# One transformer block in fp32: 256-token halves for the first weight tiles, earlier places for the scans' first chunk, and other PSUM banks in the output projections

## The chip, the core and the metric

The kernel runs on one core of a Trainium2 chip. Times are microseconds of the device for one execution. The five engines of the core are TensorE (PE, matmuls and transposes), VectorE (DVE), ScalarE (ACT), GpSimd (POOL) and SyncE (SP, which issues the transfers). Lower is better; what counts is the median of several runs.

## What is computed

The reference is one layer on 1024 tokens of width 1024, batch 1, all in float32. Each of its three sub-layers is wrapped in two RMS norms, and its result is added to the residual stream:

```
h = rms_norm(x, g_mix_pre);  proj = h @ w_in          # q, k, v of both mixers, gates, decays
attn_o = window_attention(rope(aq), rope(ak), av)     # 8 heads of 64, 2 kv heads, +-128 tokens
dn_o   = gated_deltanet(conv(dqkv), dgate, ...)       # 4 heads of 128, forward and backward scan
x = x + rms_norm(concat(attn_o, dn_o) @ w_out, g_mix_post)
c = cross_attention(rms_norm(x), rms_norm(mem), w_cq, w_ckv) @ w_co   # 4 heads of 256, 256 memory tokens
x = x + rms_norm(c, g_cross_post)
x = x + rms_norm((silu(gate) * up) @ w_down, g_ffn_post)              # gate, up = rms_norm(x) @ w_gate_up
```

## The kernel before

Float32 products are made of three matmuls of a rounded format (fp32r): every operand is split into `hi` (a cast, on ACT) and `lo` (source minus `hi`, on DVE or GpSimd), and hi\*hi, hi\*lo and lo\*hi are summed in PSUM. `split` (lines 100 to 107) makes the two halves; L103 and L104 of the profile are its cast and its subtraction, whoever calls it. `load_w` (line 119) loads one weight tile (`wraw`, 512 KB) and splits it to `whi`, `wlo`; its pool has two buffers of each. Tokens are worked on in two halves of 512 (`HALF`), each of four tiles of 128.

The order in which the engines' instructions stand is set by a scheduler from the program's order, its dependencies and its buffers. It may put matmuls of a later part between those of an earlier part, as far as their PSUM banks and weight buffers are free in program order. Each engine then works off its own list in order.

**Phase 1**, from 0 to about 368 us. Eight tiles of x are loaded (six buffers `xt`, L205; the last two when a buffer is free, L217), squared on ACT (L220), scaled on DVE (L223), transposed on PE (L228) and split to `hT`, per half `hhi` and `hlo`. `gemm_b` (L260) then multiplies weight tiles of `w_in` with `hT`, 512 tokens per matmul: 8 k-tiles of 3 matmuls for each weight tile and half. The first two weight tiles (`ws`, `pps`) are those of the DeltaNet's k. The convolution, the rotary embedding, the DeltaNet's solves (L602 to L625) and, between them, the window attention (scores `psw` L653, exponentials `sc` L662, transposes `ptw` L679, casts `ph` and differences `pl`, products `pow` L684) follow. The rotary tables `sinT` and `cosT` live in a pool of their own (`rt`); `sn` and `rot` of the rotary products in `trp`. What the scans need is written to DRAM (`d_kv`, `d_pz`, `d_gate`).

**The scans**, from about 369 to 520 us. `scan(g)` for two pairs of heads goes through eight chunks, forward and backward in the same step. Each step loads `kv` (L813, 512 KB each) and `pz` (L814, 256 KB each), two buffers of each in a pool `t3` that comes into being when phase 1 is over, and at its end `gate` (L872). Its matmuls are `psc` (L805). The rest of the window attention, the memory's norm (`mt`, squared at L911 and scaled at L914, transposed at L921, split to `mT`) and the product of `w_ckv` with it (`pck` L936, `pcv` L952) stand between the steps.

**The output projections.** `mid_gemm` (line 1019) multiplies one half of the tokens with `w_out`, later with `w_co`: twice (`ch`) 512 output columns, four token tiles `t` each with a PSUM bank of its own (`pmg`, L1036), and the weights in four pieces (`kp`). Each bank is emptied by ACT (L1039, sum of squares) and DVE (L1040, times the gain, to `z`). After both column halves every token tile is normed, added to the residual (L1050), squared (L1053) and scaled by its next norm's factor (L1056, ACT). PSUM's eight banks are here four `pg` (pool `pg3`), two `pn` (transposes) and two `px`. The calls in program order are: `w_out` on half 0, `w_out` on half 1, `cross_q` and `cross_attention` on half 0, then on half 1, `w_co` on half 0, `w_co` on half 1, and the feed-forward part (`pA` and others, L1211).

**cross_attention** (line 1105) goes through four heads. The scores of four token tiles (`pcs`, L1117, 24 matmuls of 256 columns) go to two `px` banks; DVE takes the maximum (L1119), ACT the exponentials (L1124), DVE the reciprocal and the product (L1126, L1127). Eight transposes (`pct`, L1133) go to two `pn` banks and are split to `cph`, `cpl`; twelve matmuls (`pco`, L1143) fill two `px` banks, which are split back into the operand. In the attention of half 0 the scheduler has put products of `cross_q` for half 1 (`pcq`) between these steps, in that of half 1 products of `w_co` (`pmg`), for half 0 and, beside the last heads, for half 1 as far as its k-tiles are done.

The banks of mid_gemm are claimed in one line, which is the same for both column halves:

```python
            pp = [pg.tile([P, 512], F32, tag="pg", name="pmg") for _ in range(4)]
```

## Time and profile before

| what | value |
|---|---|
| median of 3 runs | 1551.01 us (1550.01 to 1552.21) |
| the profiled execution | 1550.21 us |
| its span, first to last instruction | 1548.5 us (1.7 us lie around it) |
| mean granted PE clock | 0.991 |
| PE, DVE, ACT, POOL busy | 1491.4, 1057.6, 753.9, 364.7 us |
| moved by the transfers | 242.96 MB, 157 GB/s on average |

A timeline row gives an instruction's start, its length, engine, line, operation, tile written and tiles read, and its shape; in brackets stands how long the engine was idle ahead of it and what it waited for. Lengths of matmuls in a row overlap: a pace is read from start to start. A row of a stretch gives each engine's busy time in it, the clock that PE was granted (1.00 is full, 0.50 half), the share of time that the transfer engines were busy, and GB/s. At the start of the trace the clock column does not tell the state, the matmuls' lengths do.

### The profile page before, as it was taken

Reading aid. Unit: us, or ns where it says so; the run is one execution under the profiler, and the core shown is the slowest. Engines: PE = TensorE matmul, PEld = TensorE weight load, DVE = VectorE, ACT = ScalarE, POOL = GpSimd, SP = SyncE. Lnnn points to the kernel's source line nnn. Section 1 sums busy time; section 2 is a strip of 40 time slices with the busy share of each in tenths; the row PEclk is TensorE's granted clock in tenths of the full one; section 3 lists DMA queues with packets and bytes.
Section 4 is the critical chain, followed back from the end, with each engine's and each line's share of the span. In section 5 each row is a group of like instructions: output and inputs, shape, how many; then the busy total and the mean of one; then the engine's idle time right before and its main releaser. Section 6 shows DMA issues by size and latency. Waiting matters only on the chain. (4 is left out here: it accounts for less than half of the span.)

```text
span 1548.5 us, 21052 instructions
## 1 busy us (share of the span) xinstructions
PE 1491.4 (96%) x7451; PEld 1251.4 (81%) x7451; DVE 1057.6 (68%) x1712; ACT 753.9 (49%) x1536; POOL 364.7 (24%) x364
## 2 busy tenths in 40 slices
PE   6999999998899999999999999999999999999998
PEld 5888887777899777788888777888888888888786
DVE  6868999686798855444346368786868554696665
ACT  5578733256558865454336575332323332454532
POOL 2020200011237202053102221443533433000021
PEclk9999999999999999999999999999999999999999
DMA  6244575646997764354213254344433334853355
GB/s 205 75 116 138 157 205 136 180 138 178 338 285 250 230 227 162 99 187 144 74 55 123 88 198 143 114 131 129 150 119 120 102 103 146 292 188 102 109 175 165
DMA packets 264710, 242.96 MB, mean 157 GB/s; under 512 B 33800, under 2 KB 203677, under 8 KB 264605
## 3 DMA queue, kind: packets, MB, share of 16 engines
q1 hardware_dynamic: 264605, 241.62, 49.6%
q8 instruction: 59, 0.97, 0.3%
q14 instruction: 46, 0.38, 0.1%
HBM read 172.07 MB, written 66.88 MB: 154 GB/s over the span
## 5 line engine op out<-in xcount | busy, mean ns | idle before, releaser
L103 ACT CAST whi<-wraw 128x1024 fp32r<-128x1024 f32 x108 | 113.2, 1049 | 147.9 <-PE pmg L1036 33.9
L104 DVE TENSOR_TENSOR wlo<-wraw,whi 128x1024 fp32r<-128x1024 f32 x70 | 87.1, 1246 | 86.3 <-ACT whi L103 80.4
L260 PE MATMUL pg<-hhi,whi 128*128 128x512 f32 x352 | 140.3, 399 | 0.0
L260 PE MATMUL pg<-hlo,whi 128*128 128x512 f32 x352 | 139.6, 397 | 0.0
L260 PE MATMUL pg<-hhi,wlo 128*128 128x512 f32 x352 | 138.6, 394 | 0.0
L104 POOL TENSOR_TENSOR wlo<-wraw,whi 128x1024 fp32r<-128x1024 f32 x38 | 92.3, 2430 | 175.3 <-ACT whi L103 175.2
L1036 PE MATMUL pmg<-whi,b 128*128 128x512 f32 x384 | 119.6, 398 | 2.6 <-ACT whi L103 2.2
L1211 PE MATMUL pA<-s,whi 128*128 128x512 f32 x352 | 109.5, 392 | 1.4 <-ACT m L1228 1.4
L1036 PEld LDWEIGHTS pmg<-whi,b 128*128 128x128 f32 x384 | 71.9, 190 | 18.2 <-ACT whi L103 2.7
L1211 PEld LDWEIGHTS pA<-s,whi 128*128 128x128 f32 x352 | 65.3, 188 | 15.1 <-ACT m L1228 2.0
L1401 PE MATMUL pdX<-dhl,whi 128*128 128x512 f32 x264 | 76.1, 390 | 1.5 <-DVE zv L1456 0.8
L260 PEld LDWEIGHTS pg<-hhi,whi 128*128 128x128 f32 x352 | 66.7, 190 | 13.2 <-ACT hhi L103 0.2
L260 PEld LDWEIGHTS pg<-hhi,wlo 128*128 128x128 f32 x352 | 66.6, 189 | 13.3
L260 PEld LDWEIGHTS pg<-hlo,whi 128*128 128x128 f32 x352 | 66.6, 189 | 12.7
L1036 PE MATMUL pmg<-wlo,b 128*128 128x512 f32 x192 | 71.9, 394 | 0.0
L1288 POOL TENSOR_TENSOR act<-act,up 128x512 f32<-128x512 f32 x33 | 50.1, 1519 | 89.8 <-DVE up L1287 53.1
L1211 PE MATMUL pA<-s,wlo 128*128 128x512 f32 x176 | 68.7, 391 | 1.9 <-DVE wlo L104 1.9
L103 ACT CAST whi<-araw 128x1024 fp32r<-128x1024 f32 (+1 forms) x36 | 35.3, 982 | 70.5 <-PE pdX L1401 27.6
L104 DVE TENSOR_TENSOR wlo<-araw,whi 128x1024 fp32r<-128x1024 f32 (+1 forms) x36 | 40.7, 1132 | 38.9 <-ACT whi L103 38.8
L285 DVE SCALAR_TENSOR_TENSOR acc<-cp,cols,acc 128x1024 f32<-128x1024 f32 x48 | 62.0, 1294 | 0.1
L1401 PEld LDWEIGHTS pdX<-dhl,whi 128*128 128x128 f32 x264 | 49.3, 188 | 12.7 <-issue 1.1
L1260 POOL TENSOR_TENSOR sr<-wraw 128x512 f32<-128x512 f32 x22 | 29.4, 1336 | 124.9 <-DMA wraw<-in_w_gate_up_dram 124.2
(413 smaller groups left out, 4067.0 us busy)
## 6 DMA issues: line engine op xcount, KB each, us to landing
wraw<-in_w_gate_up_dram SPq DMA_DIRECT2D x52, 512.0 KB, 3.8
kv<-d_kv SPq DMA_DIRECT2D x32, 512.0 KB, 7.1
wraw<-in_w_in_dram SPq DMA_DIRECT2D x22, 512.0 KB, 5.5
b<-in_w_down_dram SPq DMA_DIRECT2D x20, 512.0 KB, 7.0
araw<-d_as SPq DMA_DIRECT2D x20, 512.0 KB, 3.7
pz<-d_pz SPq DMA_DIRECT2D x32, 256.0 KB, 6.5
wraw<-in_w_ckv_dram SPq DMA_DIRECT2D x16, 512.0 KB, 5.0
wraw<-in_w_out_dram SPq DMA_DIRECT2D x16, 512.0 KB, 3.9
```

What stands on the lines that cost most here:

```text
L103: nc.scalar.copy(hi, src)
L104: (eng or nc.vector).tensor_tensor(lo, src, f32(hi), ALU.subtract)
L260: nc.tensor.matmul(p_, w[:, k, :], ah[a][:, k, :], start=(k == 0 and i == 0), stop=(k == nk - 1 and i == 2))
L285: nc.vector.scalar_tensor_tensor(acc, cp[:, t:t + S], taps[t], acc, ALU.mult, ALU.add)
L1036: nc.tensor.matmul(pp[t], act[a][:, k, tt], w_[:, kk, :], start=(k == 0 and i == 0), stop=(k == KT - 1 and i == 2))
L1211: nc.tensor.matmul(out_, w[a][:, k, :], xx[b_][:, k, :], start=(start and k == 0 and i == 0), stop=(k == HK - 1 and i == 2), skip_group_ch ...
L1260: nc.gpsimd.tensor_tensor(s[0], b_[:, 0:HK], b_[:, HK:], ALU.add)
L1288: nc.gpsimd.tensor_tensor(o_, o_, up, ALU.mult)
L1401: nc.tensor.matmul(banks[t], a[:, k - k0, tt], w, start=(first and k == 0 and i == 0), stop=(k == NB - 1 and i == 2), skip_group_check=not ...
```

## The change

- The tiles `xt` have eight buffers, and all eight loads of x are issued together.
- The first two weight tiles are multiplied with half 0 of the tokens in two passes of 256 tokens, so 96 matmuls of 256 columns stand where 48 of 512 did. Half 1 is done as before.
- The rotary tables become one tile `sct` of a pool `ra` that lives through the scans, and `sn`, `rot` (and `vT`) use a tag `rr` in it. In even steps `pz` takes a place of `rr`, and in even steps of the first pair of heads `kv` takes the place of the tables; in odd steps one buffer each remains in `t3`. For the second pair of heads `kv` stays as it was.
- The loads of `gate` are ordered behind the `kv` load of the step before.
- `mid_gemm` claims its second column half's banks from `px` twice and `pg` twice, for `w_out` on half 0 from `px` twice and `pn` twice.
- L1056 becomes a multiplication on DVE (1075 in the changed file).

```diff
-    xts = [t1.tile([P, D], F32, tag="xt", name="xt", bufs=6) for _ in range(6)]
+    xts = [t1.tile([P, D], F32, tag="xt", name="xt", bufs=8) for _ in range(NT)]
...
-            gemm_b(*ws[i], hT[hf:hf + 1], [pps[i][hf]])
+            if hf:
+                gemm_b(*ws[i], hT[1:2], [pps[i][1]])
+
+        for o in (() if hf else (slice(0, 256), slice(256, 512))):
+            for i in range(2):
+                gemm_b(*ws[i], [[t[:, :, o] for t in hT[0]]], [pps[i][0][:, o]])
...
-    sinT = rt.tile([P, S], F32, name="sinT")
-    cosT = rt.tile([P, S], F32, name="cosT")
+    sct = ra.tile([P, 2, S], F32, tag="sct", name="sct")
+    sinT, cosT = sct[:, 0], sct[:, 1]
...
-            pz, kv = tl("pz", [P, 2, 2, 2, P]), tl("kv", [P, 2, 2, 4, P])
+            near = step % 2 == 0
+            pz = (ra.tile([P, 2, 2, 2, P], F32, tag="rr", name="pz", bufs=2) if near else tl("pz", [P, 2, 2, 2, P], bufs=1))
+            if g == 0:
+                kv = (ra.tile([P, 2, 2, 4, P], F32, tag="sct", name="kv") if near else tl("kv", [P, 2, 2, 4, P], bufs=1))
+            else:
+                kv = tl("kv", [P, 2, 2, 4, P])
+            before = loaded
             for d in range(2):
-                nc.sync.dma_start(kv[:, d], d_kv[g][cs[d]])
+                loaded = nc.sync.dma_start(kv[:, d], d_kv[g][cs[d]])
...
+                with tc.issue_after(before.ins):
+                    nc.sync.dma_start(gt[:, d], d_gate[rows_, cs[d] * P:(cs[d] + 1) * P]
...
+    PG, PN, PX = (pg, "pg"), (pn, "pn"), (px, "px")
+
+    def mid_gemm(tz, act, w, gp, res, dst, hf, between=None, banks=([PG] * 4, [PX] * 2 + [PG] * 2)):
...
-            pp = [pg.tile([P, 512], F32, tag="pg", name="pmg") for _ in range(4)]
+            pp = [q_.tile([P, 512], F32, tag=t_, name="pmg") for q_, t_ in banks[ch]]
...
-            nc.scalar.activation(xr, z, AF.Identity, scale=r2)
+            nc.vector.tensor_scalar(xr, z, r2, None, ALU.mult)
...
-    xn0 = mid_gemm(tz, mxT[0], w_out, gp, x, d_x1, 0)
+    xn0 = mid_gemm(tz, mxT[0], w_out, gp, x, d_x1, 0, banks=([PG] * 4, [PX] * 2 + [PN] * 2))
```

The scheduler's new order at three places. First PE's list at its very start, before: transposes of x (`ps`, L228) and the first products (L260).

```order
L228 MATMUL ps<-ident,xt 128x128 x32
L260 MATMUL pg<-hhi_142,whi 128x512 x2
L228 MATMUL ps<-ident,xt 128x128 x16
L260 MATMUL pg<-hlo_143,whi 128x512
L260 MATMUL pg<-hhi_142,wlo 128x512
L260 MATMUL pg<-hhi_142,whi 128x512
```

The same place in the changed kernel, where the two lines are 227 and 259:

```order
L227 MATMUL ps<-ident,xt 128x128 x16
L259 MATMUL pg<-hhi_146,whi 128x256
L227 MATMUL ps<-ident,xt 128x128 x8
L259 MATMUL pg<-hhi_146,whi 128x256
L259 MATMUL pg<-hlo_147,whi 128x256
L259 MATMUL pg<-hhi_146,wlo 128x256
```

Before, PE transposes four token tiles and then multiplies; now one product stands behind the second tile, and fourteen (the first three are shown) behind the third, with the fourth tile's transposes after them.

Second, ACT's list at the first steps of the scans, before. `whi` is the first weight tile of `w_ckv`, `khi` the cast of the keys' second half, `sc` the exponentials of the window attention, `ph` the cast of transposed probabilities.

```order
L835 COPY vn<-psc 128x512
L644 CAST qs<-qr 128x512
L103 CAST whi<-wraw 128x1024
L103 CAST khi<-kraw 128x1024
L662 ACTIVATE sc,ssum<-sc,nm 128x384 x4
L666 ACTIVATE es<-es 128x4
L103 CAST ph<-ptw 128x512
```

And in the changed kernel, where the lines of `vn`, `sc` and `es` are 849, 666 and 670:

```order
L103 CAST ph<-ptw 128x512
L670 ACTIVATE es<-es 128x4
L849 COPY vn<-psc 128x512
L666 ACTIVATE sc,ssum<-sc,nm 128x384 x4
L103 CAST whi<-wraw 128x1024
L868 COPY of<-psc 128x512
L103 CAST khi<-kraw 128x1024
```

The two casts have moved behind the four exponentials. A little ahead of this place, the two squares of `mt` (L911) have moved as well, from ahead of a table load and four exponentials to a place behind them and behind one more `ph`. In SP's list eight `kv` and eight `pz` loads now precede the first load of `w_ckv`, where four of each did; two of these kv and four of these pz loads stand among the last stores of phase 1.

Third, PE's list in the cross attention of half 1, at the third of its four heads, before: `pct` are the transposes of the probabilities, `pmg` the products of `w_co`.

```order
L1036 MATMUL pmg<-whi,b_6973 128x512
L1036 MATMUL pmg<-whi,b_6974 128x512
L1133 MATMUL pct<-ident,cpr 128x128 x8
L1036 MATMUL pmg<-wlo,b_6973 128x512
L1036 MATMUL pmg<-whi,b_6973 128x512
L1036 MATMUL pmg<-whi,b_6974 128x512
```

And in the changed kernel at its third head, where L1136, L1152 and L1162 are the lines of `pcs`, `pct` and `pco`:

```order
L1136 MATMUL pcs<-kr_6189,b_7589 128x256
L1136 MATMUL pcs<-kr_6190,b_7588 128x256
L1152 MATMUL pct<-ident,cpr 128x128 x8
L1162 MATMUL pco<-cph,vr_6191 128x512 x2
L1162 MATMUL pco<-cpl,vr_6191 128x512
L1162 MATMUL pco<-cph,vr_6192 128x512
```

Before, 30-odd products of `w_co` stand between a head's scores and its transposes, and some twenty between these and its output; now nothing does, for the last three of the four heads. Behind the last head 117 products of `w_co` follow in a row.

More of the change, by code (lines that the diff above doesn't have):

```diff
@@ L144, in tile_hybrid_block @@
     nega = sm.tile([P, 8], F32, name="nega")
+    ra = p12.enter_context(pool("ra", 1, side="right"))
     p1 = ExitStack()
     hx = p1.enter_context(pool("hx", 1, side="right"))
-    rt = p1.enter_context(pool("rt", 1, side="right"))
     trp = p1.enter_context(pool("trp", 2, side="right"))
@@ L198, in small @@
         return ps.tile([P, 512], F32, tag="ps", name="ps")
-    xts = [t1.tile([P, D], F32, tag="xt", name="xt", bufs=6) for _ in range(6)]
+    xts = [t1.tile([P, D], F32, tag="xt", name="xt", bufs=8) for _ in range(NT)]
     gmix = t1.tile([P, D], F32, tag="gmix", name="gmix", bufs=1)
     xload = []
-    for t in range(6):
+    for t in range(NT):
         xload.append(nc.sync.dma_start(xts[t], x[t * P:(t + 1) * P, :]))
@@ L214, in tile_hybrid_block @@
             t = 4 * hf + j
-            xt = xts[t] if t < 6 else t1.tile([P, D], F32, tag="xt", name="xt", bufs=6)
-            if t >= 6:
-                nc.sync.dma_start(xt, x[t * P:(t + 1) * P, :])
+            xt = xts[t]
             junk = t1.tile([P, D], F32, tag="junk", name="junk", bufs=1)
@@ L742, in tile_hybrid_block, with pair @@
     tl_ = p1.enter_context(pool("tl", 2))
+    def pair():
+        t = ra.tile([P, 2, HALF], F32, tag="rr", name="rr", bufs=2)
+        return t[:, 0], t[:, 1]
     def attn_proj(ct):
@@ L749, in attn_proj @@
             rop = trp.tile([P, HALF], F32, tag="rop", name="rop")
-            sn = trp.tile([P, HALF], F32, tag="rot", name="sn")
-            rot = trp.tile([P, HALF], F32, tag="rot2", name="rot2")
+            sn, rot = pair()
             nc.vector.tensor_tensor(sn, pp[hf], sinT[:, sl], ALU.mult)
@@ L764, in value_proj @@
         for hf in range(2):
-            vT = trp.tile([P, HALF], F32, tag="rot", name="vT")
+            vT = pair()[0]
             nc.scalar.copy(vT, pp[hf])
@@ L805, in mm @@
                 nc.tensor.matmul(out[:, d, h, :], lt[:, d, h, :], rt[:, d, h, :], start=True, stop=True)
-        st, first, late = None, [], None
+        st, first, late, loaded = None, [], None, None
         for step in range(NT):
```

3 lines of the change are left out of this document (1 added, 2 removed).

## The prediction

> **What bounds the kernel now.** I read the page, then TensorE's waits, then the timeline around each wait that the change touches. The page's first part:
>
> ```profile
> PE 1491.4 (96%) x7451; PEld 1251.4 (81%) x7451; DVE 1057.6 (68%) x1712; ACT 753.9 (49%) x1536; POOL 364.7 (24%) x364
> ```
>
> TensorE (PE) is busy 96% of the span, so time can come from two things alone: PE's idle time (1548.5 - 1491.4 = 57 us) and the stretches in which it runs at half clock. Which waits make up the idle time is told by PE's waits (us in total, times, longest):
>
> ```profile
> PE ps L228 <- DVE xt L223: 12.7, 4, 8.2
> PE pow L684 <- ACT ph L103: 7.3, 4, 4.0
> PE pmg L1036 <- DVE z L1040: 2.4, 1, 2.4
> PE pmg L1036 <- ACT whi L103: 2.2, 1, 2.2
> PE pA L1211 <- DVE wlo L104: 1.9, 3, 0.8
> PE pA L1211 <- ACT m L1228: 1.4, 2, 0.7
> PE pco L1143 <- ACT cph L103: 1.0, 2, 0.5
> PE pco L1143 <- DVE cpl L104: 0.8, 2, 0.6
> ```
>
> The first row is the start, the second the start of the scans, the third and fourth the output projections, the fifth and sixth the stretch right after them. The last two lie in the cross attention of the second half of the tokens. The change works at every one of these places: at the first four to remove waits, at the last, as its order of instructions shows, to add some.
>
> **The start.** PE's timeline (start, length):
>
> ```profile
> 16.13 4.03 PE L228 MATMUL ps<-ident,xt 128*128 128x128 f32 x16 [2.32 <-DVE xt L223]
> 19.99 1.22 PE L260 MATMUL pg<-hhi,whi 128*128 128x512 f32 x2
> 21.75 3.87 PE L228 MATMUL ps<-ident,xt 128*128 128x128 f32 x16 [0.54 <-DVE xt L223]
> 25.70 0.40 PE L260 MATMUL pg<-hhi,wlo 128*128 128x512 f32 x1
> 25.93 0.40 PE L260 MATMUL pg<-hhi,whi 128*128 128x512 f32 x1
> ```
>
> From 16.13 on, PE waits only 0.54 us. In the changed order one 256-token matmul stands ahead of the third token tile's transposes and fourteen behind them, so the 2.32 us wait takes one matmul (about 0.2 us) and the 0.54 us goes. The 48 matmuls of 0.23 us (25.70 to 25.93) become 96 of 0.12 (24 in 2.9 us, the row at 754.22 below): 11.5 against 11.0, a loss of 0.5. That leaves 0.3 us. At 19.99 two matmuls take 1.22 us, half speed; at 25.70 the clock is up. If PE without the 0.54 us hole gets it up one 3.4 us stretch earlier (the length of such a stretch is that of the half-clock row at 622.70 below), that is worth 1.7 more. I take half of it. The two token loads that go earlier are waited for by no PE row. **Start: 1.2 us gained**; ends -0.5 (extra instructions alone) and 2.0.
>
> **The scans' first chunk.** PE, then ACT, SP's queue, and the stretches (PE busy, PEld, DVE, ACT, POOL, granted clock, DMA share, GB/s):
>
> ```profile
> 371.42 0.49 PE L684 MATMUL pow<-ph,vhl 128*128 128x512 f32 x1 [2.00 <-ACT ph L103]
> 392.36 0.79 PE L684 MATMUL pow<-ph,vhl 128*128 128x512 f32 x1 [4.00 <-ACT ph L103]
> 394.57 0.77 PE L936 MATMUL pck<-mT,whi 128*128 128x256 f32 x2
> ```
>
> ```profile
> 371.39 1.28 ACT L662 ACT_TABLE_LOAD   x1
> 372.68 0.62 ACT L662 ACTIVATE sc<-sc,nm 128x384 f32<-128x384 f32 x1
> 375.19 1.04 ACT L103 CAST ph<-ptw 128x512 fp32r<-128x512 f32 x2
> 376.13 1.56 ACT L106 ACTIVATE mT<-ptm,cols 128x256 fp32r<-128x256 f32 x4
> 387.00 1.04 ACT L103 CAST whi<-wraw 128x1024 fp32r<-128x1024 f32 x1 [4.05 <-DMA wraw<-in_w_ckv_dram]
> ```
>
> ```profile
> 376.79 0.59 SPq L126 DMA_DIRECT2D wraw<-in_w_ckv_dram  x1
> ```
>
> ```profile
> 390.60:397.40 6.80, 5.04 (x22) 4.85 (x23) 2.94 (x8) 3.74 (x10) 0.00 (x0) 0.50 1.06 366
> 400.00:440.00 40.00, 39.02 (x315) 37.31 (x314) 35.56 (x103) 19.25 (x44) 12.44 (x9) 1.00 1.00 326
> ```
>
> The loads' sizes, from the page's DMA issues:
>
> ```profile
> kv<-d_kv SPq DMA_DIRECT2D x32, 512.0 KB, 7.1
> pz<-d_pz SPq DMA_DIRECT2D x32, 256.0 KB, 6.5
> ```
>
> ACT takes its instructions in order. It stands 4.05 us at the cast of `w_ckv`'s first tile, whose load, issued at 376.79, queues behind the scans' loads; the exponentials that PE needs stand behind that cast, so PE idles 4.00 us and then runs 6.8 us at clock 0.50. In the changed order the cast stands behind these exponentials, and the squares of `mem` behind the first ones. How early can the first `w_ckv` matmul (394.57 now) come? Ahead of the table load at 371.39 stand now two squares of 1.05 (the size of the cast at 387.00) and a `ph` of 0.5, so ACT is free for this chain at 368.8. Ahead of the cast and with it now stand a table load 1.28, eight exponentials at 0.6 (4.8), the two squares 2.1, five `ph` at 0.5, eight `mT` at 0.39, four copies of 0.5, and the cast 1.04: 16.9 us, so 385.7 if ACT never waits. I allow 2 us of waits for PE's products, 387.7. But the load comes later too: eight kv and eight pz loads, not four and four, precede it, of which two kv and four pz are issued before the last waits of phase 1. That leaves 4 MB ahead of it instead of 3, and 1 MB at 326 to 366 GB/s is 3 us. If it is issued when it is now it lands between 387 and 390; with the queue the emptier for what went early I take 388, and the matmul comes at about 389: 5.5 us earlier. From 400 on PE is busy 39.02 of 40 us, so the gain is kept. The half clock costs 1.4 us behind 394.57 now; PE's new idle time ahead of 388 puts the clock down there as well, so I count nothing. The rotary products use the new places before the loads fill them, and the load of each gate, moved behind a kv load, is needed only at the end of a step. **Scans: 5.5 us gained**; ends 0 (the loads set the pace) and 9 (5.5, the 2.00 us wait and the half clock).
>
> **The output projections.** Stretches, then ACT and DVE:
>
> ```profile
> 587.00:590.50 3.50, 3.50 (x17) 2.89 (x16) 2.31 (x3) 0.55 (x2) 0.00 (x0) 1.00 0.37 104
> 619.30:622.70 3.40, 1.17 (x6) 0.93 (x6) 1.12 (x1) 3.19 (x4) 0.13 (x1) 1.00 0.00 0
> 622.70:626.10 3.40, 3.40 (x10) 2.63 (x9) 1.24 (x2) 0.00 (x0) 0.00 (x0) 0.50 0.46 161
> ```
>
> ```profile
> 618.43 2.19 ACT L1056 ACTIVATE xr<-z,pr 128x1024 f32<-128x1024 f32 x2
> ```
>
> ```profile
> 371.28 0.75 DVE L914 TENSOR_SCALAR mt<-mt,mrs 128x1024 f32<-128x1024 f32 x1 [2.36 <-POOL mrs L161]
> ```
>
> In `w_out`'s first half the second 512 columns take px and pn, which are free, in place of pg banks that wait for L1040: 2.4 us go, less about 0.4 for a `wlo` that is next late. In its second half PE waits 2.2 us for a `whi` cast that queues behind the L1056 scalings on ACT, and 3.4 us at clock 0.50 follow, which cost 1.7. With L1056 on DVE, which is busy 1.12 of the 3.40 us, all that goes. Sixteen scalings of 0.75 cost DVE 12 us, priced at the like row L914. 2.0 + 2.2 + 1.7 = 5.9; I take **5.5 us gained**; ends 2 and 6.3. The pA waits (3.3 us) come while ACT still holds L1053 and L1056 of `w_co`'s first half; four scalings of 1.1 us leave it. **1.5 us gained**; ends 0 and 3.3.
>
> **What the banks take away.** `w_co` is what PE now does between the steps of the second half's cross attention, nearly all of it for the first half. Its second 512 columns now want px, which cross_attention uses for scores and output and which comes earlier in the program. So they cannot start until the attention is over, and the order shows three heads back to back without one other matmul. What a head takes can be read where filler hides it now:
>
> ```profile
> 754.22 3.04 PE L1117 MATMUL pcs<-kr,b 128*128 128x256 f32 x24
> 757.29 0.69 DVE L1119 TENSOR_REDUCE cmx<-pcs 128x2 f32<-128x512 f32 x1 [0.54 <-PE pcs L1117]
> 758.75 0.47 ACT L1124 ACTIVATE cpr<-pcs,cmx 128x256 f32<-128x256 f32 x1
> 759.54 0.69 DVE L1127 TENSOR_TENSOR cpr<-cpr,csum 128x512 f32<-128x512 f32 x1
> 763.24 0.60 PE L1133 MATMUL pct<-ident,cpr 128*128 128x128 f32 x4
> 764.57 1.08 ACT L103 CAST cph<-pct 128x512 fp32r<-128x512 f32 x2 [1.82 <-PE pct L1133]
> 765.18 1.29 DVE L104 TENSOR_TENSOR cpl<-pct,cph 128x512 fp32r<-128x512 f32 x2 [1.06 <-ACT cph L103]
> 772.84 0.59 ACT L103 CAST b<-pco 128x512 fp32r<-128x512 f32 x1 [0.58 <-PE pco L1143]
> ```
>
> Scores end at 757.26; maximum, exponentials and division end at 759.54 + 0.69 = 760.23: PE idles 3.0 us. Then come eight transposes, and the first `cpl` ends 0.61 + 0.69 = 1.3 us after the first `cph` starts; one matmul of 0.2 fits in: 1.1 idle. The next head's scores need the bank of the first output, split in 0.59 and about 0.7 (as for a `cpl`), 1.3 us, while the second output's six matmuls run 1.4: 0.1. That is 4.2 us a head, 12.6 for three. The pco waits of 1.0 + 0.8 that stand there now go: 10.8.
>
> The clock: 2.2 us of idle time in the 3.4 us from 619.30 were followed by 3.4 at 0.50; the 2.4 us wait that the pmg row names was not (587.00 on shows 1.00). A head's 3.0 us put it down more often than not; each time costs 1.7 less what is waiting anyway (1.1 of 3.4), about 1.0. Three heads at two chances in three: 2.0. The Trainium skill ("TensorE: Matmul & The Clock Gate", section "What's actually happening") has the clock fall only after a whole idle window of about 3.4 us. By that the heads would cost no clock and the sum would come out at 1547.3; the row at 619.30, with only 2.2 us idle, speaks against it. **Heads: 12.8 us lost**; ends 7.2 (the 3.0 alone, less 1.8) and 15.9 (4.2 + 1.7 each, less 1.8).
>
> **Sum.** 1.2 + 5.5 + 5.5 + 1.5 = 13.7 gained, 12.8 lost: 0.9 less than the profiled execution's 1550.2, so 1549.3. The runs' median is 0.8 higher; within 0.2% of it, the least that can be told from no change here, is 1547.9 to 1554.1.
>
> **The rivals.** *Faster: a head costs its first wait only.* ACT and DVE have nothing else to do there, and what I read for casts and splits may overlap transposes and products more than I allow; at 7.2 lost the sum is 13.7 - 7.2 = 6.5 gained, 1543.7. For it: the pco waits now are 0.5 us each, not 1.1. Against it: there filler stands ahead of them. *Slower: the loads set the pace of the scans.* DMA is at share 1.00 and 326 GB/s from 400 to 440, while PE is busy 39.02 of 40. If PE comes 5.5 us sooner and the kv loads of the next steps do not, each matmul on them waits, and the scan term is 0: 1549.3 + 5.5 = 1554.8. It decides once the loads finish less than about 2 us sooner than now. For it: those rows; against it: 2 of 6 MB are issued before phase 1 ends, and 2 MB are 6 us at 326 GB/s. *No half clock at the heads.* The 2.4 us wait ahead of 587.00 fell into two stretches and left the clock up; were the heads' 3.0 us cut so three times, 2.0 less is lost: 1547.3, just faster. Against it: 3.0 us cannot be cut into two halves of a 3.4 us grid without one holding 1.5, and 1.1 more idle follows. *The start does nothing*, its new order being bound as before: 1550.5, still no change.
>
> **How the numbers follow.** The cancelling sum, the empty start with it, has 0.37, with 1546.5 to 1553 as its own range; the heads at their first wait alone 0.31 and without half clock 0.05, 0.36 together for faster; the loads as the pace 0.27. Low end: 1543.7 less half of the scans' 3.5 and the clock at the start (0.8), 1541. High end: 1554.8 plus the 3.1 by which the heads may cost more, 1557.9. Outside lie two chances in ten, on both sides.
>
> **What would show it.** Right: PE waits at pct on the DVE division three times, about 3 us each, and at pco on cpl, around 840 to 875; the waits of pmg on L1040 and on `whi` gone, clock 1.00 behind them; the first pck near 389; PE matmuls with 256 columns from 16 on. Wrong: pct waits under 2 us or filler between those heads; first pck later than 392, or new psc waits on kv loads; a `whi` or `wlo` wait of like size in place of the pmg waits, now behind DVE.

## The result and the profile after

The change takes 1561.95 us (median of 4 runs, 1560.48 to 1563.66), the kernel before in the same comparison 1550.51 (1547.87 to 1552.21): a ratio of 1.0071 with the interval 1.0054 to 1.0088, so 11.0 us slower. The forecast was 1549.3 with a range up to 1557.9: wrong in sign and outside the range. The profiled execution's span is 1558.8 us, 10.3 longer than before. The page:

```profile
PE 1494.4 (96%) x7499; PEld 1255.6 (81%) x7499; DVE 1073.8 (69%) x1728; ACT 736.9 (47%) x1520; POOL 375.0 (24%) x364
```

PE is busy 3.0 us longer (48 added matmuls, and stretches at half clock), so 7.3 us of the 10.3 are new idle time. PE's waits (total, times, longest):

```profile
PE ps L227 <- DVE xt L222: 10.9, 3, 8.0
PE pct L1152 <- ACT cpr L1143: 5.0, 3, 1.7
PE pow L688 <- ACT ph L103: 4.9, 6, 2.7
PE psw L657 <- POOL qs L649: 3.0, 1, 3.0
PE pcs L1136 <- DVE b L104: 2.8, 3, 0.9
PE pct L1152 <- DVE cpr L1146: 2.4, 3, 0.8
PE pck L952 <- ACT whi L103: 2.3, 1, 2.3
PE ptn L1021 <- DVE xr L1075: 2.2, 2, 1.2
...
PE pco L1162 <- ACT cph L103: 1.4, 3, 0.5
```

The two pmg waits of before are gone, as meant. In their place stand the heads of the cross attention (pct, pcs, pco: 11.6 together), one ptn pair of 2.2, one psw of 3.0 and one pck of 2.3, while the pow row fell by only 2.4. To see where time is lost and won, I compared the moments at which PE has done the same share of all its matmul columns (columns of the trace's matmuls, a transpose's taken at three quarters; inside reordered stretches good to 1 or 2 us). A trace is of one execution, so a position can lie some us off its kernel's median. Minus is ahead of the kernel before:

| at (before's time, us) | 109 | 290 | 371 | 452 | 573 | 634 | 694 | 794 | 895 | 975 | 1520 |
|---|---|---|---|---|---|---|---|---|---|---|---|
| the change | -2.4 | +0.1 | -0.4 | +1.0 | +0.9 | -6.4 | -3.2 | -3.8 | +11.0 | +8.6 | +8.7 |

Each step of the prediction has its column: the start wins 2.4 and has lost it by 290; the scans (371 to 573) win nothing; the output projections win 7.3 and give 3.2 back; the heads (794 to 895) cost 14.8; the pA stretch wins 2.4. The rest, 1.3, is lost at the end, where the traces of all the kernels below lose 0.3 to 1.5 against the kernel before, whatever their edit.

**The start.** PE's timeline:

```profile
16.07 1.97 PE L227 MATMUL ps<-ident,xt 128*128 128x128 f32 x8 [1.11 <-DVE xt L222]
17.68 0.56 PE L259 MATMUL pg<-hhi,whi 128*128 128x256 f32 x1
...
20.82 1.39 PE L227 MATMUL ps<-ident,xt 128*128 128x128 f32 x8
21.96 0.36 PE L259 MATMUL pg<-hlo,whi 128*128 128x256 f32 x1
22.16 0.28 PE L259 MATMUL pg<-hhi,wlo 128*128 128x256 f32 x1
22.28 0.28 PE L259 MATMUL pg<-hhi,whi 128*128 128x256 f32 x1
```

From 22.16 on, 256 columns take 0.12 us from start to start: the clock is up, 3.5 us earlier than the 25.70 of before. The forecast took half of such a gain into its sum, but the earlier clock is not tied to the new start, and not worth much here. Of the eleven kernels below that keep the old start's products, seven have the clock up before 22 us in their traces. This is one of them (the scaling of `w_out`'s half 1 back on ACT):

```profile
21.66 1.07 PE L228 MATMUL ps<-ident,xt 128*128 128x128 f32 x8 [1.03 <-DVE xt L223]
23.72 1.17 PE L228 MATMUL ps<-ident,xt 128*128 128x128 f32 x8 [1.00 <-DVE xt L223]
```

Eight transposes take 1.1 us there, not 1.97, but PE then waits 1.03 and 1.00 for the token tiles where it waited 0.54. At 109 these eleven stand between -0.9 and +1.0, and the four kernels with the new start between -2.4 and -3.3. So the lead comes with the 256-token products, which PE works on while it would wait for tokens; eight buffers without them (below) give none. Two small waits at 137 to 139 give back 1.7, such as this one,

```profile
139.29 0.50 PE L479 MATMUL ps<-gm,mU_r 128*128 128x512 f32 x1 [1.18 <-ACT gm L478]
```

and the psw wait of 3.0 us, at 307.5, comes after the rest was gone.

**The scans.** SP's queue (two rows), the first cast of `w_ckv` on ACT, and the first pck on PE:

```profile
384.49 0.47 SPq L702 DMA_DIRECT2D kraw<-d_k  x1
385.74 0.56 SPq L126 DMA_DIRECT2D wraw<-in_w_ckv_dram  x1
```

```profile
394.11 1.04 ACT L103 CAST whi<-wraw 128x1024 fp32r<-128x1024 f32 x1 [3.01 <-DMA wraw<-in_w_ckv_dram]
```

```profile
395.20 0.51 PE L952 MATMUL pck<-mT,whi 128*128 128x256 f32 x2 [2.31 <-ACT whi L103]
```

The load of `w_ckv`'s first tile is issued 9 us later than before (376.79), for two reasons. The kv and pz loads that now stand ahead of it go out later (the last pz ahead of it at 380.25, against 375.25 before), and the load of `kraw` behind them waits for its place. SP's waits show the second:

```profile
SPq L702 <- PE psw L657: 3.4, 1, 3.4
```

That is 5.0 of the 9 us and 3.4 more. So the cast stands at 394.11 instead of 387.00, and pck at 395.20 instead of 394.57. It has moved behind the exponentials, and they no longer wait for it, but PE waits for it itself. The stretches before and after (columns as in the prediction), before:

```profile
370.00:400.00 30.00, 21.89 (x123) 18.63 (x124) 17.20 (x42) 18.93 (x44) 6.19 (x8) 0.83 1.04 307
```

and the changed kernel:

```profile
370.00:400.00 30.00, 23.10 (x147) 20.09 (x146) 20.83 (x57) 19.91 (x46) 7.47 (x9) 0.89 1.00 326
400.00:440.00 40.00, 37.39 (x296) 35.46 (x295) 33.32 (x89) 18.18 (x41) 12.39 (x9) 1.00 0.86 268
```

PE gains 1.2 us of work up to 400 at a higher clock, and from 400 to 440 it does 1.6 less than before's 39.02, with the transfers at 0.86 instead of 1.00: there it isn't their throughput that holds PE.

**The output projections.** The stretch that held the 2.2 us wait and the half clock, then DVE, POOL and PE about 40 us later:

```profile
619.00:626.00 7.00, 7.00 (x32) 5.79 (x32) 2.52 (x3) 2.16 (x4) 0.00 (x0) 1.00 0.47 146
```

```profile
662.43 0.74 DVE L1075 TENSOR_SCALAR xr<-z,pr 128x1024 f32<-128x1024 f32 x1
663.61 2.87 DVE L1075 TENSOR_SCALAR xr<-z,pr 128x1024 f32<-128x1024 f32 x1 [0.44 <-POOL pr L162]
```

```profile
663.55 2.38 POOL L104 TENSOR_TENSOR wlo<-wraw,whi 128x1024 fp32r<-128x1024 f32 x1
```

```profile
666.54 0.44 PE L1021 MATMUL ptn<-ident,xr 128*128 128x128 f32 x2 [1.21 <-DVE xr L1075]
```

The wait and the half clock are gone (PE busy 7.00 of 7.00). But a scaling that takes 0.74 alone takes 2.87 when it starts behind a GpSimd subtraction of 2.38, and PE's next transposes wait for it. The prediction priced all sixteen at 0.75 and off the path.

**The heads.** PE at one of the three and at the next one's scores:

```profile
820.31 3.13 PE L1136 MATMUL pcs<-kr,b 128*128 128x256 f32 x24 [0.93 <-DVE b L104]
825.12 0.63 PE L1152 MATMUL pct<-ident,cpr 128*128 128x128 f32 x4 [1.68 <-ACT cpr L1143]
826.56 0.63 PE L1152 MATMUL pct<-ident,cpr 128*128 128x128 f32 x4 [0.81 <-DVE cpr L1146]
827.64 1.22 PE L1162 MATMUL pco<-cph,vr 128*128 128x512 f32 x2 [0.46 <-ACT cph L103]
832.92 3.14 PE L1136 MATMUL pcs<-kr,b 128*128 128x256 f32 x24 [0.93 <-DVE b L104]
```

A head idles 0.93 + 1.68 + 0.81 + 0.46 = 3.9 us, against the forecast of 4.2. The place, the count and the size are right; how the idle time is made up is not (2.5 at the transposes instead of 3.0, 0.5 ahead of the output instead of 1.1, 0.9 ahead of the next scores instead of 0.1). Behind two of the three heads a stretch at half clock follows (rows in the last section).

### The profile page after: what moved, and what is told of

Read it like the earlier page. It is cut to its first block, busy times and chain, and to the rows that moved or that the text cites. A ratio compares the mean times of both kernels' runs of the same rounds, so it can differ in the third digit from the quotient of the medians.

```text
span 1558.8 us, 21137 instructions
## 1 busy us (share of the span) xinstructions
PE 1494.4 (96%) x7499; PEld 1255.6 (81%) x7499; DVE 1073.8 (69%) x1728; ACT 736.9 (47%) x1520; POOL 375.0 (24%) x364
## 4 chain that ended last, share of the span: by engine, by line
PE 73%; DVE 10%; DMA 6%; ACT 6%; SPq 2%; issue 2%; POOL 2%; DVEq 0%; POOLq 0%; ACTq 0%
PE pmg L1055 11%; PE pD L1230 8%; PE pE L1230 8%; PE pA L1230 7%; PE pdX L1420 6%; PE pg L259 5%; PE pcq L259 5%; PE pdA L1420 4%; PE pB L1230 4%; PE psc L812 3%; PE pdD L1420 2%; PE pco L1162 2%; PE pcs L1136 2%; PE pdX L1513 1%; DVE acc L284 1%
## 5 line engine op out<-in xcount | busy, mean ns | idle before, releaser
L259 PE MATMUL pg<-hhi,whi 128*128 128x512 f32 (+1 forms) x368 | 144.4, 393 | 0.6 <-ACT hhi L103 0.6
L259 PE MATMUL pg<-hlo,whi 128*128 128x512 f32 (+1 forms) x368 | 144.0, 391 | 0.0
L259 PE MATMUL pg<-hhi,wlo 128*128 128x512 f32 (+1 forms) x368 | 142.4, 388 | 0.0
L259 PEld LDWEIGHTS pg<-hhi,whi 128*128 128x128 f32 x368 | 70.6, 192 | 13.5 <-ACT hhi L103 1.0
L259 PEld LDWEIGHTS pg<-hhi,wlo 128*128 128x128 f32 x368 | 70.5, 192 | 13.0
L259 PEld LDWEIGHTS pg<-hlo,whi 128*128 128x128 f32 x368 | 70.6, 192 | 12.0
L1230 PEld LDWEIGHTS pA<-s,whi 128*128 128x128 f32 x352 | 65.5, 188 | 14.8 <-ACT m L1247 1.5
L1420 PEld LDWEIGHTS pdX<-dhl,whi 128*128 128x128 f32 x264 | 49.3, 188 | 12.8 <-issue 1.1
```

Of the source, the lines that this page charges most:

```text
L259: nc.tensor.matmul(p_, w[:, k, :], ah[a][:, k, :], start=(k == 0 and i == 0), stop=(k == nk - 1 and i == 2))
L1230: nc.tensor.matmul(out_, w[a][:, k, :], xx[b_][:, k, :], start=(start and k == 0 and i == 0), stop=(k == HK - 1 and i == 2), skip_group_ch ...
L1420: nc.tensor.matmul(banks[t], a[:, k - k0, tt], w, start=(first and k == 0 and i == 0), stop=(k == NB - 1 and i == 2), skip_group_check=not ...
```

## The experiments

Each ratio is to the kernel before, run beside it on the same chip; the gain or loss in us is the ratio on 1552. Diffs are against the kernel before where nothing else is said.

### The change with w_co's old banks on half 0

```diff
-    xn = mid_gemm(tz, q0, w_co, gp, d_x1, d_x2, 0)
+    xn = mid_gemm(tz, q0, w_co, gp, d_x1, d_x2, 0, banks=([PG] * 4, [PG] * 4))
```

(Against the change.)

> The change, but w_co on half 0 of the tokens takes four pg banks for its second 512 columns again, as before. Theory (the heads without filler cost 14.8 us, the rest of the change is a small gain): 1547, that is 14 to 16 us below the change and 2 to 5 below the kernel before. Rival (the loss sits in the moved scaling or the scans, and the heads only hide it): 1555 or more.

1551.2 us, 0.9988 [0.9979, 0.9996]: 1.9 us faster than before, 12.9 less than the change (14 to 16 were expected). The heads' waits are gone, and this one line holds more than the whole loss. The rest of the change, forecast at 13.7 gained, brings 1.9.

### The start alone

```diff
-    xts = [t1.tile([P, D], F32, tag="xt", name="xt", bufs=6) for _ in range(6)]
+    xts = [t1.tile([P, D], F32, tag="xt", name="xt", bufs=8) for _ in range(NT)]
...
+        for o in (() if hf else (slice(0, 256), slice(256, 512))):
+            for i in range(2):
+                gemm_b(*ws[i], [[t[:, :, o] for t in hT[0]]], [pps[i][0][:, o]])
```

> The kernel before with the start of the change alone (eight xt buffers, 256-token passes). Theory (PE is 2.5 us ahead at 40 us, but VectorE and ScalarE set the pace at 138 us and the window attention's q round trip at 305 us, so all is given back): no difference, 1549.5 to 1551.5, with PE ahead at 100 us and level at 330 us. Rival (the 2.5 us are a gain of their own, and other parts of the change take them back): 1548.

1559.82 us, 1.0044 [1.0028, 1.006]: 6.8 us slower. Its trace is 2.9 us ahead at 109, as the change's is, 2.3 behind at 371 and 10.0 behind at 573. So the lead and 2.3 more are given up before the scans, and the largest part, 7.7, is lost among them, 350 us behind the edit. Two of PE's waits there:

```profile
515.25 1.09 PE L808 MATMUL psc<-vn,pz 128*128 128x128 f32 x5 [2.33 <-ACT vn L838]
546.52 0.90 PE L682 MATMUL ptw<-ident,sc 128*128 128x128 f32 x3 [2.14 <-DVE m L658]
```

### The scans' places alone

```diff
+            pz = (ra.tile([P, 2, 2, 2, P], F32, tag="rr", name="pz", bufs=2) if near else tl("pz", [P, 2, 2, 2, P], bufs=1))
...
+                with tc.issue_after(before.ins):
```

> The kernel before with the scans' part alone (places of the rotary tables, gate loads behind kv loads). Theory (w_ckv's first load is issued 9 us later, behind a kraw load that waits for its buffer, so PE waits for that load instead): 1550 to 1553, no gain. Rival of the prediction (5.5 us gained once PE's place in the queue is not disturbed by the earlier start): 1545.

1551.97 us, 0.9993 [0.9982, 1.0004]: 1.1 us faster, an interval that holds no change. The first pck is late here as well (2.8 of it by what this execution was behind at 371):

```profile
398.66 0.51 PE L949 MATMUL pck<-mT,whi 128*128 128x256 f32 x2 [2.05 <-ACT whi L103]
```

### The scaling on DVE alone

```diff
-            nc.scalar.activation(xr, z, AF.Identity, scale=r2)
+            nc.vector.tensor_scalar(xr, z, r2, None, ALU.mult)
```

> The kernel before with L1056 on VectorE alone. Theory (4.2 us gained at 619, 3.2 lost at 665 where the scalings stand 2.9 us instead of 0.75 beside GpSimd's subtractions, 1.5 to 2 gained at 900): 1547 to 1549. Rival (VectorE has room for it everywhere): 1544.5.

1549.68 us, 0.9983 [0.9975, 0.9991]: 2.6 us faster.

### New banks for w_co on half 0 alone

```diff
-    xn = mid_gemm(tz, q0, w_co, gp, d_x1, d_x2, 0)
+    xn = mid_gemm(tz, q0, w_co, gp, d_x1, d_x2, 0, banks=([PG] * 4, [PX] * 2 + [PG] * 2))
```

(All other calls keep four pg banks.)

> The kernel before with the new banks in w_co on half 0 alone. Theory (the three heads without filler are the loss by themselves, about 4 us idle each and half clock after some): 11 to 14 us above the kernel before. Rival (they only cost so much together with the moved scaling and the other places): under 7 above it.

1567.19 us, 1.0099 [1.0084, 1.0115]: 15.4 us slower. PE's waits at the heads are the changed kernel's, to the tenth, though nothing else of the change is in it:

```profile
PE pct L1136 <- ACT cpr L1127: 5.0, 3, 1.7
...
PE pcs L1120 <- DVE b L104: 2.8, 3, 0.9
```

Its position goes from -1.0 at 794 to +15.3 at 895 and stays. With the first experiment the heads are settled from both sides, 12.9 and 15.4 against 12.8 forecast.

### All but the start and w_co's banks on half 0

```diff
-    xts = [t1.tile([P, D], F32, tag="xt", name="xt", bufs=8) for _ in range(NT)]
+    xts = [t1.tile([P, D], F32, tag="xt", name="xt", bufs=6) for _ in range(6)]
...
+    xn = mid_gemm(tz, q0, w_co, gp, d_x1, d_x2, 0, banks=([PG] * 4, [PG] * 4))
```

(The diff is against the change; the 256-token passes go too.)

> The change without its start (six xt buffers, 512 tokens at a time) and with w_co on half 0 on four pg banks as before; scans' places, w_out's banks and the scaling on VectorE stay. Theory (the start costs 6 to 7 us, though it is 2.5 ahead at 40 us, since the scheduler puts the scans' instructions in another order after it): 1545 to 1547, 5 to 7 us below the kernel before. Rival (the scans' places undo that loss, so that the start costs nothing in the change): as without w_co's banks, 1550 to 1552.

1546.38 us, 0.9967 [0.9954, 0.998]: 5.1 us faster than before. Beside the first experiment (1.9 faster) the start costs 3.3 in this company, but the two intervals just overlap.

### The same without the scans' places

```diff
-            pz = (ra.tile([P, 2, 2, 2, P], F32, tag="rr", name="pz", bufs=2) if near else tl("pz", [P, 2, 2, 2, P], bufs=1))
+            pz, kv = tl("pz", [P, 2, 2, 2, P]), tl("kv", [P, 2, 2, 4, P])
```

> The kernel before with w_out's new banks (and w_co's on half 1) and the scaling on VectorE; no new start, no new places, w_co on half 0 as before. Theory (each of these is a gain, the scans' places nothing): 1546 to 1548, level with the change without start and w_co banks. Rival of the prediction (the scans' places gain 5 once nothing disturbs them): 1 to 2 below the kernel before, and 4 to 5 above the run without the start.

1546.79 us, 0.9963 [0.995, 0.9975]: 5.7 us faster. So banks and scaling bring 5.7, of which the scaling alone had 2.6; the scans' places add nothing. The slow scaling stands here as in the change: 2.86 us on DVE from 665.01, behind a subtraction of 2.37 on POOL from 664.95.

### Eight token buffers alone

```diff
-    xts = [t1.tile([P, D], F32, tag="xt", name="xt", bufs=6) for _ in range(6)]
+    xts = [t1.tile([P, D], F32, tag="xt", name="xt", bufs=8) for _ in range(NT)]
...
-            xt = xts[t] if t < 6 else t1.tile([P, D], F32, tag="xt", name="xt", bufs=6)
-            if t >= 6:
-                nc.sync.dma_start(xt, x[t * P:(t + 1) * P, :])
+            xt = xts[t]
```

> The kernel before with eight xt buffers alone, which touches two loads and no product at the start, but after which the scheduler orders the scans' part differently (295 of 350 PE rows of one stretch stand elsewhere). Theory (the other order of the scans is what costs in the start's part): 2 to 7 us above the kernel before, lost between 370 and 580. Rival (it is the 256-token passes themselves): within 1 us of the kernel before.

1563.77 us, 1.0077 [1.0064, 1.0089]: 12.0 us slower, for two loads issued earlier. PE's position is -0.2 at 109, 0 at 290, +1.3 at 371, +8.3 at 452 and +18.1 at 573 (the traced execution is the slowest of five, 3.1 above the median). PE's waits and two of their rows:

```profile
PE pow L682 <- ACT ph L103: 13.4, 7, 5.4
```

```profile
394.94 0.80 PE L682 MATMUL pow<-ph,vhl 128*128 128x512 f32 x1 [5.40 <-ACT ph L103]
457.81 0.50 PE L682 MATMUL pow<-ph,vhl 128*128 128x512 f32 x1 [3.02 <-ACT ph L103]
```

The pow row was 7.3 in four waits before. The order of PE's matmuls in the two traces shows the same place: apart from a few shifts in the first 62 us it is the same up to the twelfth pck, the 1900th of 7451 (397 us); of the next 1281, 904 stand elsewhere; from 595 us on it is the same again to the end, buffer numbers left out. In the same way the start alone differs at the beginning, where its passes are, and then from 382 to 574 us. Nearly all of the time is lost where the order differs, and the 256-token passes are not needed for it.

### The scaling of w_out's half 1 back on ACT

```diff
-            nc.vector.tensor_scalar(xr, z, r2, None, ALU.mult)
+            if on_act:
+                nc.scalar.activation(xr, z, AF.Identity, scale=r2)
+            else:
+                nc.vector.tensor_scalar(xr, z, r2, None, ALU.mult)
```

(Against the kernel without start and scans' places; `on_act` is set for `w_out` on half 1 alone.)

> w_out's new banks and the scaling on VectorE without the start, the scans' places and w_co's banks on half 0, but on half 1 of w_out the scaling stays on ScalarE. Theory (there the scalings last 2.9 us beside GpSimd's subtractions and PE waits 2.2 us, 3.2 with what follows): 3 us below the same kernel with all scalings on VectorE, 1543 to 1544.5, and no ptn wait near 665. Rival (ScalarE's own queue would be late there now that PE comes sooner): no difference, 1546 to 1547, with a whi wait in place of the ptn wait.

1542.27 us, 0.9933 [0.992, 0.9946]: 10.4 us faster than before, 4.7 better than with all scalings on DVE, with the intervals apart, and the ptn waits are gone. That is more than the 2.4 that those waits made; by position the kernel with all scalings on DVE loses 3.6 between 634 and 694, this one 0.1.

### cross_q's differences on DVE instead of GpSimd

```diff
-            whi, wlo = load_w(w_cq[:, ct * P:(ct + 1) * P], KT, P, nc.gpsimd)
+            whi, wlo = load_w(w_cq[:, ct * P:(ct + 1) * P], KT, P)
```

(Against the kernel without start and scans' places, all scalings on DVE.)

> The same kernel with all scalings on VectorE, and with the subtractions of cross_q's weights on VectorE, not GpSimd. Theory (the scalings are long because both engines work at once, not because VectorE has too much to do): the two scalings of 2.9 us take 0.75, the ptn waits at 665 shrink below 0.5 us each, 1543.5 to 1545. Rival (VectorE has too much to do): the ptn waits stay or grow, 1546.5 or more.

1543.86 us, 0.9945 [0.993, 0.996]: 8.5 us faster than before; its interval meets that of the kernel it was made from. The scalings, unchanged themselves, are short again, and PE's ptn wait is gone:

```profile
665.83 0.75 DVE L1059 TENSOR_SCALAR xr<-z,pr 128x1024 f32<-128x1024 f32 x1 [0.44 <-POOL pr L161]
...
668.23 0.74 DVE L1059 TENSOR_SCALAR xr<-z,pr 128x1024 f32<-128x1024 f32 x1
```

So it was GpSimd's subtraction that made them long. The Trainium skill ("SBUF — State Buffer", section "Who interferes with whom") says that a VectorE `tensor_scalar` can run in a mode in which it wants the pair of ports shared with GpSimd, and that whoever comes second is blocked for the other's whole instruction. The rows agree to within 0.2 us: in the changed kernel 663.55 + 2.38 is 665.93, and the scaling, 0.74 long when alone, ends 0.55 behind that.

### w_ckv's first tile loaded ahead of the scans

```diff
+    first_ckv = [load_w(w_ckv[:, 0:P], KT, P, nc.gpsimd)]
     scans = [scan(g) for g in range(2)]
...
-        whi, wlo = load_w(w_ckv[:, ct * P:(ct + 1) * P], KT, P, nc.gpsimd)
+        whi, wlo = first_ckv.pop() if first_ckv else load_w(w_ckv[:, ct * P:(ct + 1) * P], KT, P, nc.gpsimd)
```

(Against the kernel with all but the start and `w_co`'s banks on half 0.)

> The run without the start (scans' places in), but with the first tile of w_ckv loaded ahead of all the scans' loads. Theory (what kept the scans' places from gaining is that load's place in SP's queue, 9 us later than in the kernel before): PE's wait for whi near 393 is gone, 2 to 4 us below the run without the start, 1542.5 to 1544.5. Rival (the transfers or the chain of the scans' steps set the pace, whichever load comes first): no difference, 1545.5 to 1547.5.

1542.08 us, 0.9928 [0.9914, 0.9943]: 11.2 us faster than before, 6 better than without the early load and 5.5 better than with neither early load nor places, in both cases with no overlap of the intervals. That is the size that the prediction gave to the scans. How it comes about is not shown. The wait that the theory wants gone is not there in the trace without the early load: its first tile is issued at 385.47, and yet PE reaches the first pck with no idle time ahead of it.

```profile
393.37 0.40 PE L949 MATMUL pck<-mT,whi 128*128 128x256 f32 x2
```

By position PE wins some 3 us on the kernel before from 371 to 573 with the early load, and loses 1 without it; from 370 to 400 PE is busy 26.11 us at clock 0.94 with it, and 24.45 at 0.89 without. (The traced execution is the slowest of six, 3.8 above the median, and was 5 behind at 371 already.)

### All that helped

```diff
+    first_ckv = [load_w(w_ckv[:, 0:P], KT, P, nc.gpsimd)]
...
+            if on_act:
+                nc.scalar.activation(xr, z, AF.Identity, scale=r2)
```

(Scans' places, early load, `w_out`'s banks, the split scaling, `w_co` on half 0 with its old banks, the start as before.)

> All that gained, together: scans' places, w_ckv's first tile ahead of the scans' loads, w_out's new banks, w_co's banks on half 0 as before, the scaling on VectorE except on half 1 of w_out; no new start. Theory (the gains lie in different stretches and add up): 1538 to 1540, 13 to 15 below the kernel before. Rival (ahead by more, the next part of the program is what sets the pace): 1541 to 1543, as each of them alone.

1539.59 us, 0.9923 [0.9908, 0.9938]: 12.0 us faster than before, the lowest median of all, though its interval overlaps those of the early load and of the split scaling. On top of the split scaling, places and early load bring 1.6 here, not 5.5. PE's waits begin

```profile
PE ps L229 <- DVE xt L224: 14.1, 5, 8.3
PE pow L685 <- ACT ph L103: 3.8, 4, 2.7
```

with no pck, ptn, pct or pmg row among the ten largest. In the stretch that the scans' term is about it has

```profile
370.00:400.00 30.00, 26.18 (x167) 21.98 (x166) 21.42 (x56) 22.41 (x52) 6.52 (x9) 0.94 1.00 310
```

against 21.89 at 0.83 before. The pow wait of 2.7 that is left at 378 stands behind a table load and four exponentials on ACT.

### The early load without the places

```diff
-            pz = (ra.tile([P, 2, 2, 2, P], F32, tag="rr", name="pz", bufs=2) if near else tl("pz", [P, 2, 2, 2, P], bufs=1))
+            pz, kv = tl("pz", [P, 2, 2, 2, P]), tl("kv", [P, 2, 2, 4, P])
```

(Against the kernel with the early load.)

> w_ckv's first tile ahead of the scans' loads, but with the scans' places as in the kernel before; w_out's new banks and all scalings on VectorE. Theory (the early load is a gain with the places, since only then the scans' first loads start before phase 1 ends): 1546 to 1548, as without either. Rival (the early load is the whole gain, the places nothing): 1541 to 1543, as with both.

1549.55 us, 0.9984 [0.9974, 0.9994]: 2.5 us faster than before, 8.7 worse than with the places and 3.2 worse than without the early load, where the intervals just overlap. Each of the two edits alone brings nothing or loses; both together bring 5.5.

### The best one with the start

```diff
-    xts = [t1.tile([P, D], F32, tag="xt", name="xt", bufs=6) for _ in range(6)]
+    xts = [t1.tile([P, D], F32, tag="xt", name="xt", bufs=8) for _ in range(NT)]
```

(And the 256-token passes.)

> All that gained together, and the start of the change added. Theory (the start is worth 2.5 us by itself and costs what the new order of the scans makes of it, so its price changes with that order): anything from 3 us below to 8 above the run without it, with PE 2.5 us ahead at 100 us in either case and the rest of the difference between 230 and 560. Rival (the 256-token passes and the two early loads cost 6 to 7 us as such): 6 to 7 us above it.

1548.74 us, 0.9979 [0.997, 0.9989]: 8.7 us worse than without the start, intervals apart. That is a little more than the theory allowed, and too near the rival's 6 to 7 to tell the two by size. The place speaks for the theory: PE is 4.3 us ahead of the kernel without the start at 109 and still at 371, and 5.6 behind it at 573 (the traced execution is the fastest of twelve, 4.1 below the median). PE's list differs at the beginning and from 382 to 591 us, and the waits of the start alone are back:

```profile
508.78 1.16 PE L812 MATMUL psc<-vn,pz 128*128 128x128 f32 x8 [2.35 <-ACT vn L849]
538.32 1.12 PE L683 MATMUL ptw<-ident,sc 128*128 128x128 f32 x4 [2.14 <-DVE m L659]
```

PE's position, against the kernel before, of the kernels that matter most:

| at (before's time, us) | 109 | 371 | 452 | 573 | 634 | 694 | 794 | 895 | 975 | 1520 |
|---|---|---|---|---|---|---|---|---|---|---|
| eight buffers alone | -0.2 | +1.3 | +8.3 | +18.1 | +16.6 | +16.5 | +16.5 | +16.5 | +16.2 | +16.2 |
| w_co banks, half 0, alone | -0.9 | +0.5 | +1.3 | +1.3 | -1.0 | -1.0 | -1.0 | +15.3 | +15.3 | +15.3 |
| banks and scaling | +0.5 | +1.3 | +1.7 | +1.9 | -5.4 | -1.8 | -2.5 | -2.4 | -4.5 | -4.5 |
| all that helped | +1.0 | +2.3 | -1.9 | -2.9 | -9.6 | -9.5 | -9.5 | -9.4 | -11.8 | -11.9 |
| the same with the start | -3.3 | -2.0 | -4.1 | +2.7 | -4.6 | -4.6 | -4.6 | -4.6 | -7.0 | -7.0 |

## Why the prediction was wrong

Term by term, in us (minus is a gain). The first experiment, the sixth and the change itself split the loss, by construction without a rest: -5.1 for all but the start and the heads, +3.3 for the start, +12.9 for the heads, together +11.0.

| term | forecast | measured |
|---|---|---|
| start | -1.2 | +3.3 in the change, +6.8 alone, +8.7 in the best one |
| scans' first chunk | -5.5 | -1.1 alone, +0.6 between two kernels: none |
| output projections and pA | -7.0 | -5.7 |
| heads | +12.8 | +12.9 in the change, +15.4 alone |

**The start: the step that failed is "The two token loads that go earlier are waited for by no PE row", and with it the price of a step by its own place.** That sentence is true of the place where the loads stand; what failed is that it put them at nothing for the whole program. The local part came out larger than forecast, 2.4 us ahead at 109 instead of 1.2, and partly for another reason: 0.85 of the 1.2 were for an earlier clock, which kernels with the old start have as well without being ahead. But the scheduler builds one order for the whole program, and the eight buffers, which nobody near them waits for, changed the order of the scans: 12.0 us lost alone, nearly all of it where the order differs. The order of the changed kernel could be read before the run; I read in it the three places that the terms were about, and gave the start no chance of costing more than 0.5. Why the scheduler's new order is the worse one is not shown: its planned times shift at the start, and what it decides from 390 us on comes out otherwise, is argued only. No kernel had the start with the old order behind it, so it isn't shown that the order is the cause and doesn't merely differ where the loss is; and why the sizes 3.3, 6.8, 8.7 and 12.0 differ is open.

**The scans: the step that failed is "If it is issued when it is now it lands between 387 and 390".** It was issued at 385.74 instead of 376.79, and the first pck came at 395.20 instead of 389, beyond the 392 that the prediction named as a sign of being wrong. I had counted the loads ahead of it in bytes, not their turns and waits in SP's list: 5.0 us are those loads', 3.4 the wait of the load of `kraw` for its place. I had walked ACT's list for the cast, and not SP's for the load that the cast needs. That this lateness is what kept the whole gain away is not shown: in the run of all but the start and `w_co`'s banks the load is as late and PE has no wait for it, and still the places bring nothing. Places and early load together bring 5.5, the forecast's size, with the reason open.

**The output projections were right in mechanism, a little large in size.** The waits and the half clock went (7.3 by position against 5.9 worked out), and 3.2 came back as long scalings beside GpSimd's subtractions. "Priced at the like row L914" was the term mis-sized: 0.75 holds only where GpSimd isn't subtracting, 2.87 where it is. Two kernels that take away either side of that pair gain 4.7 and 2.8 over the one that has both (for the 2.8 the intervals meet).

**The heads were right**, in place, number and size, the half clock behind two of three too.

**The rivals.** "The loads set the pace of the scans" (slower, 1554.8) named the right place and the right result for that term, but from 400 to 440, where it had the transfers set the pace, they were at 0.86 and not at 1.00. From 370 to 400 they are at 1.00 or more in both kernels, and what they hold up there is not shown. It would have been 7 us short even so, since neither it nor the range had a start that costs. "The start does nothing" was the closest case on the start, and still on the wrong side. "Heads at their first wait only" and "no half clock at the heads" are refuted by the rows above.

**What stays open**: how the start's cost in the change itself (3.3, intervals just overlapping) divides into waits; by what wait the scans' places cost without the early load what they bring with it; why the kernel with all that helped is 12.0 below before, where 5.5 for places and early load and 4.7 for the split scaling on top of 5.7 would make 16; and the last 1.3 us of the change's loss at 1541 to 1546, which no experiment addressed.

## What to carry to other kernels

Where a scheduler makes the order, an edit is not local: compare the whole order list with the old one, and give every stretch in which it differs a term or at least a range, also those hundreds of microseconds behind the edit. When a load is moved, walk its queue and ask of every transfer ahead of it what that one waits for, before counting bytes. Independent work between dependent steps is worth the idle time that it hides (3.9 us a head here); before giving a bank to an earlier user, see which such work loses it.

## What the runs showed of the hardware

The granted clock fell after less idle time than the whole of a stretch. In each of the sixteen traces the moments at which it falls lie whole multiples of 3.413 us apart, to 0.001 us. Cut on that grid, the changed kernel's stretches around the heads are these (PE busy in the second column):

```profile
810.00:813.42 3.42, 1.85 (x16) 1.64 (x14) 2.36 (x6) 1.56 (x7) 0.00 (x0) 1.00 0.00 0
813.42:816.83 3.41, 2.04 (x11) 1.19 (x11) 1.66 (x4) 1.55 (x5) 0.00 (x0) 1.00 0.00 0
...
823.66:827.07 3.41, 1.14 (x8) 0.84 (x8) 2.18 (x6) 1.48 (x7) 0.00 (x0) 1.00 0.00 0
827.07:830.49 3.42, 2.96 (x9) 2.22 (x8) 1.29 (x2) 1.01 (x2) 0.00 (x0) 0.50 0.00 0
...
837.31:840.73 3.42, 1.72 (x10) 1.13 (x10) 1.63 (x4) 1.87 (x6) 0.00 (x0) 1.00 0.02 5
840.73:844.14 3.41, 3.41 (x9) 2.49 (x8) 0.80 (x2) 0.00 (x0) 0.00 (x0) 0.50 0.00 0
```

2.27 and 1.70 us idle of 3.41 were each followed by half clock, 1.57 was not. Over all sixteen traces (from 60 to 1500 us, stretches at full clock), all 46 stretches with 1.9 us idle or more were followed by half clock, 8 of 11 with 1.7 to 1.9, 16 of 69 with 1.2 to 1.7 and 3 of 100 with 0.9 to 1.2. So more idle time made it likelier, as the prediction's two chances in three took it, and between 1.2 and 1.9 the idle time of a stretch does not alone decide it. The Trainium skill ("TensorE: Matmul & The Clock Gate", section "What's actually happening") wants a whole idle window for the clock to fall; these rows disagree with it, and the measurement decides.

A DVE scaling of 128 x 1024 took 0.74 to 0.75 us alone and 2.86 to 2.87 when it started 0.06 us behind a GpSimd subtraction of 2.37 to 2.38, in two kernels. And two loads issued earlier, which cost PE nothing where they stand, went with a loss of 12.0 us some 350 us later, where the scheduler's order differs.
